# Expert weights loaded as 256 rows of 1024 columns in place of 1024 rows of 256

## Chip, core and metric

The kernel runs on one core of a Trainium2 chip. The metric is the time of one execution on the device in microseconds. The engines are PE (TensorE: matmuls, with PEld for its weight loads), DVE (VectorE), ACT (ScalarE), POOL (GpSimd) and SP (SyncE, which issues most transfers).

## The reference

One decoder layer for 1024 tokens of width 1024: a mixer (attention beside gated linear attention), and then a feed-forward part in which a router sends each token to 4 of 32 experts. The change is in the experts alone:

```python
def expert_block(args):
    xb, e = args
    u = xb @ w_mlp1[e] + b_mlp1[e]
    x_glu = jnp.minimum(u[..., ::2], SWIGLU_LIMIT)
    x_lin = jnp.clip(u[..., 1::2], -SWIGLU_LIMIT, SWIGLU_LIMIT)
    a = x_glu * jax.nn.sigmoid(SWIGLU_ALPHA * x_glu) * (x_lin + 1)
    return a @ w_mlp2[e] + b_mlp2[e]
```

`w_mlp1[e]` is 1024 x 2048 and `w_mlp2[e]` is 1024 x 1024, both float32: 8 MB and 4 MB an expert, 384 MB for all 32. The results are weighted by the gates and summed over a token's experts.

## The kernel before

All up to about 551 us is the mixer, the router and the lists of tokens. Then comes the expert stage, up to 1972 us, and a tail that finishes the rows.

An expert's tokens are gathered from memory by POOL (L1079, `xg`), turned by PE (`pxh`, L1071) and copied by ACT and DVE into `xTh` and `xTl`, the high and the low fp16 piece of the turned tokens. Each expert has a fixed number of token slots, from 368 down to 60 (`CAPS`); large and small experts take turns (`ORDER`).

The weights come in pieces of 1 MB through `piece` (L1044). It loads 1024 rows by 256 columns into a staging tile `st` of [128, 8, 256] floats, so that one partition receives eight runs of 256 floats (1 KB each). Seven staging tiles take turns. Each is split into two fp16 tiles of [128, 8, 256]: ACT writes the high piece `eh` (L168) and DVE the low piece `el`, the weight less its high piece (L169). Both work by half a tile, 128x1024 elements, so a load has two splits on each engine. Eight pairs of `eh` and `el` take turns.

```python
        return (nc.scalar.activation(dh, src, AF.Copy, scale=SW),
                nc.vector.scalar_tensor_tensor(dl, src, SW, dh, op0=OP.mult, op1=OP.subtract))
```

One pair of pieces serves 48 matmuls: 2 outputs by 8 contraction tiles by the 3 products of `mm3` (L149 to L151). In the first layer (`up`) eight pieces an expert give `pu`, from which ACT makes `gl` (L1115) and `sg` (L1117), DVE makes `lin` in three steps (L1119 to L1121), and POOL splits that into `aTh` and `aTl`. In the second layer (`down`) four pieces give `pyv`, which ACT copies to `yT` (L1146, L1148); later PE turns it, ACT scales it by the gates into `yo` (L1160), and POOL adds it to the rows of the result by an indirect transfer (L1163).

The second layer of expert i follows the first layer of expert i+1, and the turning of tokens and results goes between the pieces of the first layer. So 12 pieces with few slots (a `down` and an `up`) and 12 with many take turns.

A scheduler sets the order of each engine's instructions when the kernel is built; on the chip each engine runs in that order and waits where it must. A load is issued by SP when the staging tile that it takes has been read by both splits of its last use; a split waits for its load and for the last matmul that reads the pair of tiles it overwrites.

Of the kernel before, what the change touches and what calls it, by code (L numbers as in the profile page):

```python
# [19 lines left out]
T = 1024  # L20
D = 1024
# [5 lines left out]
SLOTS = 1152            # slot-table rows of one expert (1024 tokens at most, and one block of padding)  # L27
DUMP = 512              # rows that unused slots add zeros to, each slot of an expert's blocks to another

SW = 2048.0             # weights are split into fp16 pieces of SW * w  # L30
SX = 16.0               # activations into pieces of SX * x
SA = 256.0              # expert activations into pieces of SA * a
# [4 lines left out]
# slots per expert, by the expert's place in the order of their loads; what does not fit goes  # L37
# through the loop over overflow blocks
# [3 lines left out]
# a large and a small expert by turns, and pairs of many slots beside pairs of few; the first has two blocks  # L42
# [7 lines left out]
def layer_kernel(  # L50
# [39 lines left out]
    # ---------------------------------------------------------------- constants  # L90
# [18 lines left out]
    mt = consts.tile([128, 32], F32, name="mt")      # expert ids along the free axis  # L109
# [4 lines left out]
    cnt = consts.tile([128, NE], F32, name="cnt")    # tokens of each expert so far, on every partition  # L114
# [11 lines left out]
    pr = consts.tile([64, 2, NE], F32, name="pr")    # experts by rank, loads by rank  # L126
    Pf = consts.tile([64, NB], F32, name="Pf")       # one-hot of each block's expert
    bi = consts.tile([NB, 1], I32, name="bi")

    def rstd_from(ss, dst, width, m=128):  # L130
        """dst = (ss / width + eps) ** -0.5"""
        nc.scalar.activation(dst, ss, AF.Ln, bias=epsc[:m], scale=1.0 / width)
        nc.scalar.activation(dst, dst, AF.Exp, scale=-0.5)

    def rms(ss, rs, t2, m, after=()):
        """rs = (ss / D + eps) ** -0.5, with a step of Newton's"""
# [10 lines left out]
    def mm3(ps, sh, sl, mh, ml, first, last):  # L147
        """ps += (sh + sl)^T (mh + ml), all but the product of the two low parts"""
# [4 lines left out]
    hTh = mixer.tile([128, 8, T], F16, name="hTh")   # pieces of h, then of the heads' outputs, feature-major  # L153
# [4 lines left out]
    # pieces of q and k: those of key head g's queries on top of one another beside the key's high piece twice  # L158
# [12 lines left out]
    # ---------------------------------------------------------------- pass 1: modulation, input projection  # L171
    with tc.tile_pool(name="p1", bufs=1) as p1, tc.tile_pool(name="stage", bufs=4) as stage, \
# [4 lines left out]
        # rows -> columns: c, b_ada, g_pre_mix, g_post_mix, g_pre_ffn, g_post_ffn, g_gla_norm  # L177
# [11 lines left out]
        # silu(c)  # L189
# [9 lines left out]
        # x / rms(x), feature-major, in the places of q and of the GLA's q and k  # L199
# [23 lines left out]
        # shift1 and scale1 as columns, two at a time; s1 = (1 + scale1) g SX, sh1 = shift1 SX  # L223
# [11 lines left out]
        def ada_columns(pc):  # L235
# [8 lines left out]
            # the sums over the partitions' 8 rows: shift1's by TensorE, scale1's by VectorE  # L244
# [22 lines left out]
        def modulate(pc):  # L267
            """h = x / rms(x) * s1 + sh1 in two fp16 pieces"""
# [28 lines left out]
        def queries(p):  # L297
            # heads 2p, 2p+1 beside heads 2p+4, 2p+5: partitions 0-63 carry key head 0, 64-127 key head 1
# [22 lines left out]
        def first_queries(pc):  # L321
            """what features 256 pc to 256 pc + 255 of h add to the queries of heads 0, 1, 4 and 5"""
# [49 lines left out]
        # k, v and the low-rank gate  # L372
# [36 lines left out]
    # ---------------------------------------------------------------- pass 2: attention and GLA, by token tile  # L409
# [3 lines left out]
    # w_out: rows of attention heads i and i+4 make contraction tile i  # L413
# [622 lines left out]
    with tc.tile_pool(name="stB", bufs=7, reuse_waits="tile") as stB, tc.tile_pool(name="sp", bufs=8, reuse_waits="tile") as sp, \  # L1036
# [53 lines left out]
        def up(n, w1e, bc, xT, tag, behind=(), between=(), lead=None, wp=None):  # L1090
# [4 lines left out]
            for j in range(8):  # L1095
                with ExitStack() as es:
                    for ins in behind[:2 * j]:
                        es.enter_context(tc.issue_after(ins))
# [374 lines left out]
```

## Time and profile before

| | us |
|---|---|
| time, median of 3 runs | 2048.79 (2048.52 to 2051.15) |
| span of the profiled execution | 2046.8 |
| PE busy | 1858.8 (91%) |
| DVE busy | 1545.4 (76%) |
| ACT busy | 1307.3 (64%) |
| POOL busy | 984.7 (48%) |
| splits on DVE (L169, `el`), 768 | 936.5 |
| splits on ACT (L168, `eh`), 768 | 797.6 |
| weight loads (L1047), 384 of 1 MB | 73.7% of the DMA engines' span, with all else on their queue |

The profiled execution's own time is its span, and the table shows the median of the runs beside it. An engine's busy share is over the whole span, of which the expert stage is some two thirds; a window is a stretch of the span, with the busy time of each engine in it, the clock that TensorE was granted (1.00 is full) and the share of the DMA engines' time that packets took. That share can come out above 1.

### The profile page before, as it was taken

What the parts mean: (1) busy time and instruction counts of PE and PEld (TensorE: products, weight loads), DVE (VectorE), ACT (ScalarE), POOL (GpSimd) and SP (SyncE); (2) the same over time, 40 slices, a digit from 0 to 9 for tenths busy, and PEclk for the clock granted to TensorE, in tenths of its full rate; (3) what the DMA queues carried; (4) which work ended last, traced back from release to release, by engine and by line L of the source; (5) the groups of instructions that cost most, each with busy time, mean ns of one, the idle gap of its engine ahead of it and who ended that gap; (6) DMA issues with size and microseconds to landing.
All of it is one profiled execution on the core that took longest, in us unless ns stands there. A gap on an engine that the chain in (4) does not pass through costs nothing. (4 is left out here: it accounts for less than half of the span.)

```text
span 2046.8 us, 55660 instructions
## 1 busy us (share of the span) xinstructions
PE 1858.8 (91%) x22929; PEld 1596.1 (78%) x22929; DVE 1545.4 (76%) x2518; ACT 1307.3 (64%) x2248; POOL 984.7 (48%) x986
## 2 busy tenths in 40 slices
PE   6999999988598999989989999999999999899971
PEld 3456777655387999989989997779889999889970
DVE  6814555666679989988988996679687978969863
ACT  5524444433366868777777885678577768858760
POOL 2205765736645556545544563336344435734432
PEclk9999999999788999989999999999999999999985
DMA  8412322343399999999999999699999999999993
GB/s 287 147 45 83 94 73 83 93 151 125 135 335 320 337 330 330 339 324 337 320 312 344 337 329 331 191 316 330 312 290 308 346 298 311 327 303 313 310 278 103
DMA packets 493381, 525.94 MB, mean 257 GB/s; under 512 B 19071, under 2 KB 472969, under 8 KB 493090
## 3 DMA queue, kind: packets, MB, share of 16 engines
q1 hardware_dynamic: 474432, 476.40, 73.7%
q0 software_dynamic: 17392, 41.72, 8.7%
q8 instruction: 181, 2.97, 0.6%
q10 hardware_dynamic: 1298, 4.21, 0.5%
q14 instruction: 78, 0.64, 0.1%
HBM read 482.50 MB, written 39.76 MB: 255 GB/s over the span
## 5 line engine op out<-in xcount | busy, mean ns | idle before, releaser
L169 DVE SCALAR_TENSOR_TENSOR el<-st,eh 128x1024 f16<-128x1024 f32 x768 | 936.5, 1238 | 113.5 <-ACT eh L168 110.7
L168 ACT ACTIVATE eh<-st 128x1024 f16<-128x1024 f32 x768 | 797.6, 1054 | 284.2 <-PE pu L150 142.6
L149 PE MATMUL pu<-xTh,eh 128*128 128x232 f16 (+31 forms) x4096 | 781.8, 232 | 10.2 <-issue 4.9
L151 PE MATMUL pu<-xTh,el 128*128 128x232 f16 (+31 forms) x4096 | 781.1, 231 | 8.3 <-issue 8.2
L150 PE MATMUL pu<-xTl,eh 128*128 128x232 f16 (+31 forms) x4096 | 780.8, 231 | 4.0 <-issue 3.6
L150 PEld LDWEIGHTS <-eh 128*128 128x128 f16 x6080 | 598.8, 99 | 67.9 <-issue 46.0
L149 PEld LDWEIGHTS <-eh 128*128 128x128 f16 x6080 | 596.5, 99 | 32.5 <-issue 10.5
L151 PEld LDWEIGHTS <-el 128*128 128x128 f16 x6080 | 596.2, 99 | 29.3 <-issue 7.5
L1122 POOL CAST aTh<-lin 128x232 f16<-128x232 f32 (+31 forms) x256 | 294.0, 1148 | 538.9 <-DVE lin L1121 493.4
L149 PE MATMUL pyv<-aTh,eh 128*128 128x232 f16 (+30 forms) x1984 | 382.2, 234 | 32.6 <-ACT yT L1148 30.6
L150 PE MATMUL pyv<-aTl,eh 128*128 128x232 f16 (+30 forms) x1984 | 381.8, 233 | 2.7 <-issue 2.6
L151 PE MATMUL pyv<-aTh,el 128*128 128x232 f16 (+30 forms) x1984 | 381.7, 233 | 1.3 <-issue 1.3
L1123 POOL TENSOR_TENSOR aTl<-lin,aTh 128x232 f16<-128x232 f32 (+31 forms) x256 | 251.2, 981 | 20.7
L1119 DVE TENSOR_SCALAR lin<-pu,bt 128x232 f32<-128x232 f32 (+31 forms) x256 | 110.0, 430 | 93.5 <-PE pu L151 62.6
L1163 POOL DMA_INDIRECT yacc<-yo,tokI x52 | 94.0, 1808 | 119.1 <-ACT yo L1160 113.2
L636 POOL TENSOR_TENSOR st<-st,sil 128x512 f32<-128x512 f32 x64 | 68.3, 1068 | 150.3 <-DMA st<-in_w_ada_dram 149.7
L1115 ACT ACTIVATE gl<-pu,bt 128x232 f32<-128x232 f32 (+31 forms) x256 | 97.3, 380 | 55.4 <-PE pu L151 44.3
L1120 DVE SCALAR_TENSOR_TENSOR lin<-lin,bt,sg 128x232 f32<-128x232 f32 (+31 forms) x256 | 104.2, 407 | 14.2 <-issue 0.2
L1117 ACT ACTIVATE sg<-gl,c 128x232 f32<-128x232 f32 (+31 forms) x256 | 107.5, 420 | 1.1
L1079 POOL DMA_INDIRECT xg<-h2d,gatI x50 | 71.9, 1438 | 43.2 <-DVE gcol L1239 20.1
L1121 DVE SCALAR_TENSOR_TENSOR lin<-gl,lin 128x232 f32<-128x232 f32 (+31 forms) x256 | 84.9, 332 | 4.3
L151 PE MATMUL pb<-wvh,hTl 128*128 128x256 f16 x256 | 70.7, 276 | 0.0
(402 smaller groups left out, 2479.2 us busy)
## 6 DMA issues: line engine op xcount, KB each, us to landing
st<-in_w_mlp_dram SPq DMA_DIRECT2D x384, 1024.0 KB
st<-in_w_ada_dram SPq DMA_DIRECT2D x64, 256.0 KB
xt<-in_x_dram SPq DMA_DIRECT2D x16, 512.0 KB
st<-in_w_ada_dram SPq DMA_DIRECT2D x16, 512.0 KB
st<-in_w_in_dram SPq DMA_DIRECT2D x7, 1024.0 KB
x1d<-xt SPq DMA_DIRECT2D x8, 512.0 KB
h2d<-h2s SPq DMA_DIRECT2D x8, 512.0 KB
yacc<-yi ACTq DMA_DIRECT2D x8, 512.0 KB
```

What stands on the lines that cost most here:

```text
L149: nc.tensor.matmul(ps, sh, mh, start=first, stop=False)
L150: nc.tensor.matmul(ps, sh, ml, start=False, stop=False)
L151: return nc.tensor.matmul(ps, sl, mh, start=False, stop=last)
L168: return (nc.scalar.activation(dh, src, AF.Copy, scale=SW), nc.vector.scalar_tensor_tensor(dl, src, SW, dh, op0=OP.mult, op1=OP.subtract))
L169: nc.vector.scalar_tensor_tensor(dl, src, SW, dh, op0=OP.mult, op1=OP.subtract))
L1115: nc.scalar.activation(gl, pu[0], AF.Relu, scale=-SG, bias=bc(0, j))
L1117: sgs.append(nc.scalar.activation(sg, gl, AF.Sigmoid, scale=-1.702 * INV / SG, bias=c7))
L1119: nc.vector.tensor_scalar(lin, pu[1], bc(1, j), bc(2, j), op0=OP.max, op1=OP.min)
L1120: nc.vector.scalar_tensor_tensor(lin, lin, bc(3, j), sg, op0=OP.add, op1=OP.mult)
L1122: nc.gpsimd.tensor_copy(aTh[:, j, :], lin)
L1123: lows.append(nc.gpsimd.tensor_tensor(aTl[:, j, :], lin, aTh[:, j, :], op=OP.subtract))
L1163: end["dma"] = nc.gpsimd.indirect_dma_start(out=yacc, out_offset=bass.IndirectOffsetOnAxis(ap=si(b)[:m, :], axis=0), in_=yo[:m, :], in_off ...
```

## The change

`piece` becomes `pieces`, which loads a group of four pairs at once. Each of its four loads fetches 256 rows by 1024 columns into a staging tile of [128, 2, 1024] floats: two runs of 1024 floats (4 KB each) for a partition. Each load holds a quarter of the rows for all four pairs, so it is split into four parts, 128x512 elements each, one for each pair. A group has the same 4 MB and the same four loads, with 16 splits on each engine in place of 8, and a pair is complete when all four loads are in. The numbers of staging tiles (7) and of pairs (8) stay.

`up` calls `pieces` for its pieces 0 to 3 and again for 4 to 7, `down` once. The pieces taken ahead of the first tokens are a whole group where they were one piece. The staging tile is also borrowed for the first-layer biases (`b1f`) and for rows of the tail (`xys`), in its new shape. The matmuls are the same, in number and in shape.

```diff
-        def piece(src):
-            st = stB.tile([128, 8, 256], F32, name="st")
-            loads.append(nc.sync.dma_start(st, src.rearrange("o (k p) f -> p (o k) f", p=128)))
-            wh = sp.tile([128, 8, 256], F16, name="eh")
-            wl = sp.tile([128, 8, 256], F16, name="el")
-            for hh in range(2):
-                ks = slice(hh * 4, hh * 4 + 4)
-                splits.append(split(wh[:, ks, :], wl[:, ks, :], st[:, ks, :]))
-            return wh, wl
+        def pieces(src, j):
+
+            ws = [(sp.tile([128, 8, 256], F16, name="eh"), sp.tile([128, 8, 256], F16, name="el")) for _ in range(4)]
+            for kq in range(4):
+                st = stB.tile([128, 2, 1024], F32, name="st")
+                rows = src[:, kq * 256:(kq + 1) * 256, j * 1024:(j + 1) * 1024]
+                loads.append(nc.sync.dma_start(st, rows.rearrange("o (k p) f -> p (o k) f", p=128)))
+                ks = slice(kq * 2, kq * 2 + 2)
+                for c, (wh, wl) in enumerate(ws):
+                    splits.append(split(wh[:, ks, :], wl[:, ks, :], st[:, :, c * 256:(c + 1) * 256]))
+            return ws
...
-                    wh, wl = wp if wp and j == 0 else piece(w1e(j))
+                if j % 4 == 0:
+                    with ExitStack() as es:
+                        for ins in behind[:2 * j]:
+                            es.enter_context(tc.issue_after(ins))
+                        ws = wp if wp and j == 0 else pieces(w1e(j), j // 4)
+                wh, wl = ws[j % 4]
...
+                if half == 0:
+                    ws = pieces(w2e, 0)
                 for q in range(2):
-                    wh, wl = piece(w2e(half * 2 + q))
+                    wh, wl = ws[half * 2 + q]
...
-        wp = piece(w1[ds(e[0], 1), :, 0:256])
+        wp = pieces(w1[ds(e[0], 1)], 0)
...
-            b1f = stB.tile([128, 8, 256], F32, name="st")[0:NE].rearrange("p a n -> p (a n)")
+            b1f = stB.tile([128, 2, 1024], F32, name="st")[0:NE].rearrange("p a n -> p (a n)")
```

The order moves in three places that matter below. The names in brackets are the queues and engines that a row waits for. First, ACT at the start of the expert stage, where the first expert's first pieces stand beside its tokens, before:

```order
L168 ACTIVATE eh<-st 128x1024 [waits DMAHW2_49,DVE_49]
L168 ACTIVATE eh<-st 128x1024
L1075 ACTIVATE xTh<-pxh 128x8x128 [waits PE_49]
L1075 ACTIVATE xTh<-pxh 128x8x104 [waits PE_49]
L168 ACTIVATE eh<-st 128x1024 [waits DMAHW5_49,Pool_49]
L168 ACTIVATE eh<-st 128x1024
```

and after:

```order
L168 ACTIVATE eh<-st 128x512 [waits DMAHW2_49,DVE_49]
L168 ACTIVATE eh<-st 128x512 [waits DMAHW5_49,Pool_49]
L168 ACTIVATE eh<-st 128x512
L168 ACTIVATE eh<-st 128x512 [waits DMAHW7_49]
L168 ACTIVATE eh<-st 128x512 [waits DMAHW4_49]
L168 ACTIVATE eh<-st 128x512 x3
L168 ACTIVATE eh<-st 128x512 [waits DMAHW5_49]
L168 ACTIVATE eh<-st 128x512 x3
L168 ACTIVATE eh<-st 128x512 [waits DMAHW6_49]
L168 ACTIVATE eh<-st 128x512 x3
L1076 ACTIVATE xTh<-pxh 128x8x128 [waits PE_49]
L1076 ACTIVATE xTh<-pxh 128x8x104 [waits PE_49]
```

Two splits stood ahead of the two copies of the tokens (`xTh`), and now 16 stand there, four for each of four loads, load by load (the waits for DMAHW2, 4, 5 and 6 at the head of each four).

Second, ACT in the first layer of the expert with 112 slots, at its first three pieces, before:

```order
L168 ACTIVATE eh<-st 128x1024 [waits DMAHW5_49,PE_49]
L1115 ACTIVATE gl<-pu,bt 128x112 [waits DVE_49,PE_49]
L1160 ACTIVATE yo<-pxy,gcol 92x512 [waits DMASW6_49,PE_49]
L1117 ACTIVATE sg<-gl,c_78 128x112 [waits Activation_49]
L168 ACTIVATE eh<-st 128x1024
L168 ACTIVATE eh<-st 128x1024 [waits DMAHW6_49,PE_49]
L1115 ACTIVATE gl<-pu,bt 128x112 [waits DVE_49,PE_49]
L1160 ACTIVATE yo<-pxy,gcol 92x512 [waits PE_49]
L1117 ACTIVATE sg<-gl,c_78 128x112 [waits Activation_49]
L168 ACTIVATE eh<-st 128x1024
L168 ACTIVATE eh<-st 128x1024 [waits DMAHW7_49,PE_49]
L1115 ACTIVATE gl<-pu,bt 128x112 [waits DVE_49,PE_49]
```

and after:

```order
L168 ACTIVATE eh<-st 128x512 [waits DMAHW5_49,PE_49]
L1118 ACTIVATE gl<-pu,bt 128x112 [waits DVE_49,PE_49]
L1165 ACTIVATE yo<-pxy,gcol 92x512 [waits DMASW6_49,PE_49]
L1120 ACTIVATE sg<-gl,c_78 128x112 [waits Activation_49]
L168 ACTIVATE eh<-st 128x512 [waits DMAHW6_49]
L168 ACTIVATE eh<-st 128x512 [waits DMAHW7_49]
L1118 ACTIVATE gl<-pu,bt 128x112 [waits DVE_49,PE_49]
L1165 ACTIVATE yo<-pxy,gcol 92x512 [waits PE_49]
L1120 ACTIVATE sg<-gl,c_78 128x112 [waits Activation_49]
L168 ACTIVATE eh<-st 128x512 x3
L168 ACTIVATE eh<-st 128x512 [waits DMAHW0_49]
L1118 ACTIVATE gl<-pu,bt 128x112 [waits DVE_49,PE_49]
```

Where each piece had one load to wait for, the first loads of the group come at once, the second pair's splits of them next, and the split that waits for the fourth load (DMAHW0) follows only after these, with two rounds of `gl` and `sg` in between.

Third, ACT in the first layer of the expert with 216 slots, at the same place, before:

```order
L168 ACTIVATE eh<-st 128x1024 [waits DMAHW1_49,PE_49]
L1115 ACTIVATE gl<-pu,bt 128x216 [waits DVE_49,PE_49]
L1160 ACTIVATE yo<-pxy,gcol 128x512 [waits DMASW3_49,PE_49]
L1117 ACTIVATE sg<-gl,c_78 128x216 [waits Activation_49]
L168 ACTIVATE eh<-st 128x1024
L168 ACTIVATE eh<-st 128x1024 [waits DMAHW2_49,PE_49]
```

and after:

```order
L168 ACTIVATE eh<-st 128x512 [waits DMAHW1_49,DVE_49,PE_49]
L1118 ACTIVATE gl<-pu,bt 128x216 [waits PE_49]
L1165 ACTIVATE yo<-pxy,gcol 128x512 [waits DMASW3_49,PE_49]
L1120 ACTIVATE sg<-gl,c_78 128x216 [waits Activation_49]
L168 ACTIVATE eh<-st 128x512 [waits DMAHW2_49]
L168 ACTIVATE eh<-st 128x512 [waits DMAHW3_49]
L168 ACTIVATE eh<-st 128x512 [waits DMAHW4_49]
L168 ACTIVATE eh<-st 128x512 [waits DVE_49,PE_49]
L1118 ACTIVATE gl<-pu,bt 128x216 [waits PE_49]
```

Here the first pair's four splits, of all four loads (DMAHW1 to 4), follow one another, with no other split between.

## Rows read from the trace of the kernel before

**Rows 1.** The page: the span and the queue of all weight loads.

```profile
span 2046.8 us, 55660 instructions
...
q1 hardware_dynamic: 474432, 476.40, 73.7%
```

**Rows 2.** Windows by pair of experts: start and end, length, busy us (instructions) per engine, clock, share.

```profile
core 0: us, PE busy (x) PEld busy (x) DVE busy (x) ACT busy (x) POOL busy (x), PEclk, DMA share, GB/s
568.80:666.90 98.10, 87.94 (x1045) 83.44 (x1045) 84.09 (x145) 65.92 (x91) 48.03 (x39) 0.89 1.09 328
666.90:745.80 78.90, 74.50 (x1227) 73.98 (x1225) 73.43 (x99) 64.46 (x97) 45.31 (x38) 0.98 1.09 332
745.80:831.60 85.80, 84.58 (x1228) 84.01 (x1226) 74.30 (x100) 64.49 (x97) 44.77 (x38) 1.00 1.08 332
831.60:916.00 84.40, 76.60 (x1227) 76.04 (x1225) 74.17 (x99) 64.52 (x97) 43.51 (x38) 0.94 1.07 330
...
998.20:1084.50 86.30, 77.36 (x1227) 76.81 (x1225) 74.86 (x101) 64.62 (x97) 40.95 (x38) 0.96 1.07 322
...
1166.40:1248.00 81.60, 78.68 (x1243) 77.88 (x1241) 74.28 (x100) 65.42 (x98) 48.33 (x39) 1.00 1.09 338
1248.00:1366.70 118.70, 116.43 (x1228) 82.08 (x1226) 77.64 (x101) 69.36 (x103) 38.32 (x38) 0.99 0.86 271
1366.70:1442.40 75.70, 73.08 (x1265) 72.15 (x1264) 72.27 (x100) 66.12 (x101) 48.45 (x41) 0.98 1.05 315
...
1548.80:1623.90 75.10, 72.05 (x1267) 71.03 (x1266) 71.46 (x99) 65.89 (x101) 47.11 (x41) 1.00 1.05 320
...
1719.30:1804.10 84.80, 75.38 (x1234) 74.67 (x1233) 73.06 (x99) 65.59 (x99) 49.33 (x39) 0.94 1.05 317
...
sum 1403.70, PE 1336.62 PEld 1259.77 DVE 1186.13 ACT 1045.65 POOL 692.11; mean PE 83.54 PEld 78.74 DVE 74.13 ACT 65.35 POOL 43.26
```

**Rows 3.** Windows: loads of x in rows of 4 KB, then of weights in rows of 1 KB.

```profile
10.00:14.00 4.00, 3.50 (x16) 2.59 (x14) 2.45 (x7) 3.74 (x10) 0.00 (x0) 1.00 0.99 393
...
826.00:844.00 18.00, 18.00 (x229) 17.97 (x227) 14.48 (x17) 12.20 (x18) 4.36 (x4) 1.00 1.10 348
```

**Rows 4.** Timeline of ACT, 896 to 912: start, duration, instruction, idle before it.

```profile
897.16 1.06 ACT L168 ACTIVATE eh<-st 128x1024 f16<-128x1024 f32 x1 [5.46 <-DMA st<-in_w_mlp_dram]
...
902.21 1.06 ACT L168 ACTIVATE eh<-st 128x1024 f16<-128x1024 f32 x1 [2.53 <-DMA st<-in_w_mlp_dram]
```

**Rows 5.** Timeline of PE, 905 to 907.

```profile
906.57 0.30 PE L149 MATMUL pyv<-aTh,eh 128*128 128x168 f16 x1 [7.37 <-ACT yT L1148]
```

**Rows 6.** Waits of the DMA queue of SP: who for whom, us, times, longest.

```profile
SPq L1047 <- DVE el L169: 588.9, 217, 8.5
```

**Rows 7.** Instructions of line 169 (DVE), duration ns least, median, most.

```profile
L169 DVE SCALAR_TENSOR_TENSOR el<-st,eh x768: 1190/1218/1902, 559.3 to 1968.4; 128x1024 f16<-128x1024 f32 x192
...
L169 DVE SCALAR_TENSOR_TENSOR wol<-wo,woh x16: 639/844/1527, 186.2 to 404.1; 128x512 f16<-128x512 f32 x16
```

**Rows 8.** Instructions of line 168 (ACT), likewise.

```profile
L168 ACT ACTIVATE eh<-st x768: 1039/1054/1109, 558.2 to 1965.2; 128x1024 f16<-128x1024 f32 x192
...
L168 ACT ACTIVATE woh<-wo x16: 629/630/632, 167.6 to 379.4; 128x512 f16<-128x512 f32 x16
```

**Rows 9.** Timeline of ACT at the start of the expert stage.

```profile
563.49 1.02 ACT L1075 ACTIVATE xTh<-pxh 128x1024 f16<-128x1024 f16 x1 [3.32 <-PE pxh L1071]
567.89 0.86 ACT L1075 ACTIVATE xTh<-pxh 128x832 f16<-128x832 f16 x1 [3.38 <-PE pxh L1071]
...
571.79 2.00 ACT L168 ACTIVATE eh<-st 128x1024 f16<-128x1024 f32 x2 [1.15 <-DMA st<-in_w_mlp_dram]
```

**Rows 10.** Timeline of PE, 558 to 568.8.

```profile
566.98 1.57 PE L1071 MATMUL pxh<-identh,xg 104*128 104x104 f16 x16 [2.68 <-DMA xg<-h2d,gat]
```

**Rows 11.** Timeline of SP at the start of the program.

```profile
1.58 6.29 SPq L316 DMA_DIRECT2D xt<-in_x_dram  x8
```

**Rows 12.** Timeline of ACT at the start of the program.

```profile
5.28 1.06 ACT L209 ACTIVATE junk<-xt 128x1024 f16<-128x1024 f32 x1 [3.26 <-DMA xt<-in_x_dram]
```

More of the change, by code (lines that the diff above doesn't have):

```diff
@@ L1095, in up @@
             for j in range(8):
-                with ExitStack() as es:
-                    for ins in behind[:2 * j]:
-                        es.enter_context(tc.issue_after(ins))
-                    wh, wl = wp if wp and j == 0 else piece(w1e(j))
+                if j % 4 == 0:
[4 more added lines that the diff above has]
+                wh, wl = ws[j % 4]
                 if n <= 256:
@@ L1196, in piece_of @@
                         e[1] = expert(i, perm1)
-                return w1[ds(e[min(j, 1)], 1), :, j * 256:(j + 1) * 256]
+                return w1[ds(e[min(j, 1)], 1)]
             return up(CAPS[r], piece_of,
@@ L1304, in layer_kernel @@
             _, si, gc = args(ORDER[i])
-            yTs = down(n, lambda q: w2[ds(e[1], 1), :, q * 256:(q + 1) * 256], aT)
+            yTs = down(n, w2[ds(e[1], 1)], aT)
             left = combine(n, yTs, si, gc)
@@ L1315, in layer_kernel @@
         aTh, aTl = up_of(i, e, xT[i][0])
-        wps = [piece(w2[ds(e[1], 1), :, q * 256:(q + 1) * 256]) for q in range(4)]
+        wps = pieces(w2[ds(e[1], 1)], 0)
         with tc.issue_after(sgs[-1].ins):
@@ L1333, in layer_kernel @@
             if t < NT - 2:
-                st = stB.tile([128, 8, 256], F32, name="st").rearrange("p a n -> p (a n)")
+                st = stB.tile([128, 2, 1024], F32, name="st").rearrange("p a n -> p (a n)")
                 xys.append((st[:, 0:D], st[:, D:2 * D]))
@@ L1426, in layer_kernel @@
             run(steps)
-            aTo = up(128, lambda j: w1[ds(e, 1), :, j * 256:(j + 1) * 256],
+            aTo = up(128, lambda j: w1[ds(e, 1)],
                      lambda q, j: bto[:, q, j, :], xTo, "B")
-            yTo = down(128, lambda q: w2[ds(e, 1), :, q * 256:(q + 1) * 256], aTo)
+            yTo = down(128, w2[ds(e, 1)], aTo)
             run(combine(128, yTo, lambda b: ti[:, 0:1], lambda b: gx))
```

## The prediction

> **What bounds the kernel now.** I read the page's busy shares, then the windows of the expert stage pair by pair, then the waits, and at last single instructions. The span is 2046.8 us [rows 1]; the median of the runs is 2048.8, so 2.0 us lie around the span. The change touches only the expert weights, so 0 to 551 us (the mixer) and the tail after 1972 us stay as they are.
>
> The expert stage alternates an expert of many slots with one of few, and it repeats every two experts, so a window holds one such pair: 24 loads of 1 MB, 48 splits on ACT and 48 on DVE, and 24 pairs of pieces for PE. The 16 windows make 1403.7 us, of which PE is busy 1336.6 [rows 2]: PE idles 67 us, and where it has idled its clock falls, which the granted clock shows (0.89, 0.94, 0.96). The loss by the clock is (1 − clock) × length. Four windows are **starved** (78.9, 84.4, 86.3 and 84.8 us, 334.4 together): PE idles 4.4, 7.8, 8.9 and 9.4 us = 30.6 in them and loses 1.6 + 5.1 + 3.5 + 5.1 = 15.3 by the clock. Four **middle** ones (82 to 86 us, the first and the last are shown) idle 0.7 to 2.9, 7.6 in all. The others are heavy (PE is the bound), follow a heavy one, or are the first and the last.
>
> What starves PE is the weight DMA. Its share stands at 1.05 to 1.09 in the starved windows [rows 2], and at 348 GB/s with 1.10 in a stretch without a pause [rows 3]: 316 GB/s for each unit of share. The page gives the same: 476.40 MB in 73.7% of 2046.8 us is 316 GB/s, or 3.32 us of all engines for one 1 MB load [rows 1]. 24 × 3.32 = 79.7 us is about the length of the starved windows. Just ahead of such a stop, ACT waits 5.46 and 2.53 us for `st` before a split [rows 4], and PE then stands 7.37 us [rows 5]; the profile names `yT`, but ACT was done with splits just before, and the weights are the late party. DVE is busy 73.1 to 74.9 us of the same windows [rows 2]: it is the next bound, close behind.
>
> **The change, part by part.**
>
> *Transfer.* Rows of 1 KB become rows of 4 KB. The trace has those: x is loaded in rows of 4 KB, at 393 GB/s with a share of 0.99 [rows 3], 397 GB/s, 2.64 us for 1 MB. I take 2.64 (3.32 is the other end, if the pitch between the rows should cost what their length saves). A window then needs 24 × 2.64 = 63.4 us for weights in place of 79.7, and its share falls to about 0.86. The DMA is no longer the bound.
>
> [...]
>
> *Splits.* A group of four pairs took 8 splits of 128x1024 on each of DVE and ACT and takes 16 of 128x512. On DVE 128x1024 takes 1190 ns at least (median 1218), and 128x512, in the mixer, 639 at least (median 844) [rows 7]. Two small for one large cost 2 × 639 − 1190 = 88 ns more, 48 times in a window: **+4.2 us**. With the 28 ns that the median of the large one stands over its minimum on each instruction, 116 ns: +5.6. With the median of the small ones, 2 × 844 − 1218 = 470 ns: +22.6; that is an upper bound, since those 16 ran beside other work of the mixer, and I take the lower. DVE in a starved window goes from 73.9 (mean of the four) to 78.1 to 79.5. On ACT: 2 × 629 − 1054 = 204 ns [rows 8] × 48 = +9.8 at most, 65 → 75, which lies under DVE's.
>
> [...]
>
> *So DVE takes the DMA's place.* DVE also idles a little: in the windows that follow a heavy one, 75.7 and 75.1, it idles 3.4 and 3.6 [rows 2]. Between 78.1 + 0 and 79.5 + 3.5 I take 81 us for each starved window.
>
> *Order.* A pair of pieces now needs all four loads of its group. The loads of a group are let go together: with 7 staging buffers the fourth load of the next group goes into the buffer of this group's first, which is free only when the last pair's split of it is done. SP waits 588.9 us for `el` already, without harm where loads are queued ahead [rows 6]. I cost this at 0, since while the load is away DVE has the last pair's other splits and the next group's first ones to do; the price without that cover is rival C.
>
> *Start.* In the first group the order stands load by load, and all 16 splits stand ahead of both copies of the first tokens. Now the copies end at 568.75 and the first product follows at 568.8. The third load's split started at 571.79 [rows 9], with 3.25 MB landed (the biases too). The fourth: 571.79 + 0.75 × 2.64 − 2 × (3.32 − 2.64) = 572.4. Then four splits of ACT (2.5), a copy (1.02), the transposes of the second block (half of 1.57 [rows 10], whose 16 operations are eight for each piece), its copy (0.86): first product about 577.5, **8.7 us later**. The first window idles 10.2 us and loses 10.8 by the clock; with a whole group ready that should shrink by about as much. DVE allows an earlier end: its 84.09 us of the window, 2.4 for the two splits that now run before it and 5 for the price above, less the 16 × 0.64 = 10.2 us of splits that are done by 574.9, leave 81.3, and 3 idle make 659 against 666.9. So the term lies between −8 and +8.7; I take 0.
>
> *Sum.* Starved: 4 × 81 = 324 against 334.4: −10.4. Middle: half of their 7.6: −4. Heavy, after heavy, last: 0, since PE bounds them or eight pairs stand ready. First: 0. Span 2046.8 − 14 = 2032, plus 2.0 around it makes 2034, rounded up to **2035 us**.
>
> **The rivals.**
>
> *B, full relief.* DVE's idle vanishes, since splits run ahead in heavy windows, and PE bounds all. The four give back 30.6 + 15.3, the middle 7.6 and the first 6: 59.5, so **1989**. For it: eight pairs of pieces can be ready ahead, and DVE could work for the next window while PE is the bound in a heavy one. Against: eight are a third of a window's 24, and in the four PE alone would need 70 to 74 us (its busy time less the loss by the clock), less than DVE's 78.
>
> *C, slower: the fourth load's round trip.* Load to load: x's first 512 KB was issued at 1.58 and used at 5.28, 3.7 us [rows 11, 12], of which 1.3 is the transfer at 2.64 a MB; so 2.4 + 2.64 = 5.0 for a whole load, plus 0.6 for ACT's split: 5.6. DVE's cover, where its order goes straight on (the 216 slots in the order shown), is three splits of the old group and three of the new: 6 × 0.64 = 3.8. It then stops 1.8 us a group, six groups a window: 79 + 10.8 = 90. Eight windows (the starved and the middle, 666 us) become 718: +52, **2101**; where it stops in half of the groups, 8 × 84.4 = 675: +9, 2058. It decides from 0.7 us a group, where 79 + 6 × 0.7 reaches their mean of 83.2. Against: in the expert of 112 slots the second pair's three splits stand ahead of the fourth load's, 9 × 0.64 = 5.8, which covers it. For: only one spare load of room, and ACT's and PE's part in the chain is not counted.
>
> *D, no change.* The price is 136 ns a pair of splits, not 88: 73.9 + 6.5 + 3.5 = 84, 4 × 84 = 336 against 334: **2049**.
>
> *E, it doesn't load faster.* The rows of one load are 8 KB apart in memory for the first layer. Then 24 × 3.32 stays, with DVE at 79 beside it: between D and C; its chance is in theirs.
>
> **How the numbers follow.** A measurement of this kernel tells 0.2%, 4 us, from no change. Forecast (DVE the bound, 5 to 35 us gained): 0.44. B: 0.16. C, whole or half: 0.28. D: 0.12. Faster: the forecast less 0.04 that falls under 4 us or turns out a loss, plus B: 0.56. Same: D and half of that 0.04: 0.14. Slower: C and the other half: 0.30. The range reaches from B's value, 1988, to 2078, between C's half and its whole; some 0.1 is left out on either side.
>
> **What would show it.** Right: share of DMA under 0.95 in the starved windows, weights at 380 GB/s or more for each unit of share; DVE busy 78 to 80 us in them with 128x512 at 640 to 670 ns; PE idle less than now, clock at 0.97 or more. C: splits on ACT waiting for `st` once a group, on the fourth load, and SP waiting for `el` right before it. Start: first product near 577. Wrong altogether: DVE's 128x512 at over 700 ns, or the load still at 3.3 us.

## The result, and the profile after

The changed kernel takes **2146.1 us** (median of 4 runs, 2134.4 to 2148.1) against 2048.7 us before: a ratio of 1.046, 95% interval 1.043 to 1.049. The forecast was 2035 us with a range up to 2078. It is slower, and by more than the rival that ended on this side.

The page of the changed kernel, lines that answer to [rows 1] and to the busy times in the table ahead (the groups of instructions: busy time, mean ns | idle time before them and what ended most of it):

```profile
span 2145.8 us, 57143 instructions
...
PE 1884.6 (88%) x22929; PEld 1612.4 (75%) x22929; DVE 1616.1 (75%) x3286; ACT 1373.8 (64%) x3016; POOL 917.7 (43%) x986
...
q1 hardware_dynamic: 179520, 476.40, 63.5%
...
L169 DVE SCALAR_TENSOR_TENSOR el<-st,eh 128x512 f16<-128x512 f32 x1536 | 1026.8, 711 | 132.3 <-ACT eh L168 129.4
L168 ACT ACTIVATE eh<-st 128x512 f16<-128x512 f32 x1536 | 875.4, 622 | 330.5 <-DMA st<-in_w_mlp_dram 209.9
```

The transfers did get shorter: 63.5% of 2145.8 us for the same 476.40 MB is 350 GB/s for each unit of share (316 before), 3.00 us for a 1 MB load in place of 3.32. The splits cost about what was reckoned: DVE 1026.8 us in place of 936.5, ACT 875.4 in place of 797.6. What is new stands behind the bar of the last line: ACT now idles before its splits mostly for the weight loads.

The same pairs of experts as in [rows 2], seven of the 16 lines, and the sum:

```profile
593.80:686.80 93.00, 85.67 (x1044) 81.78 (x1044) 80.84 (x184) 63.45 (x131) 42.76 (x39) 0.91 0.88 304
686.80:771.20 84.40, 74.24 (x1227) 73.69 (x1225) 75.52 (x144) 66.04 (x141) 38.71 (x38) 0.98 0.95 319
771.20:865.70 94.50, 86.66 (x1227) 85.22 (x1225) 82.54 (x153) 71.40 (x150) 33.81 (x38) 0.96 0.90 305
865.70:955.60 89.90, 76.22 (x1228) 75.79 (x1226) 78.06 (x147) 69.02 (x145) 44.23 (x37) 0.94 0.90 302
...
1046.00:1130.50 84.50, 79.01 (x1226) 78.28 (x1224) 77.11 (x146) 68.06 (x144) 34.86 (x38) 0.96 0.94 317
...
1428.90:1512.10 83.20, 74.06 (x1266) 72.37 (x1264) 74.79 (x143) 67.20 (x143) 50.36 (x40) 0.98 0.92 306
...
1810.20:1897.60 87.40, 76.94 (x1235) 76.22 (x1233) 74.84 (x141) 65.89 (x140) 44.13 (x39) 0.92 0.90 296
...
sum 1482.20, PE 1352.26 PEld 1270.85 DVE 1249.72 ACT 1109.11 POOL 627.68; mean PE 84.52 PEld 79.43 DVE 78.11 ACT 69.32 POOL 39.23
```

The share of DMA has fallen below 0.96 in all of them, to 0.90 to 0.95 in the starved ones, where the forecast had about 0.86, and yet all of the 16 but the first and the one from 1046.0 are longer. By the groups of the prediction: starved 334.4 → 346.2 (+11.8), middle 331.5 → 361.7 (+30.2), first 98.1 → 93.0 (−5.1), and the seven that it costed at nothing (heavy, after heavy, last) 639.7 → 681.3 (+41.6); together +78.5. The first product starts at 593.8 in place of 568.8, of which 13.1 us lie after the first slots' numbers are known (28.6 us from there, 15.5 before). The other 11.9 lie in the mixer, whose instructions are the same, in the same order; in the profiles of this study it ends anywhere between 546 and 565 us, for kernels that share it. The tail gave back 4.5. 78.5 + 13.1 + 11.9 − 4.5 is the 99.0 between the spans. From the first slots' numbers to the end, which leaves the mixer out, the profile takes 1580.6 us in place of 1493.5.

The waits of 600 us to the end (who <- for whom: us, times, longest), before and then after:

```profile
ACT eh L168 <- DMA st<-in_w_mlp_dram: 65.3, 47, 6.8
...
PE pyv L149 <- ACT yT L1148: 30.6, 9, 7.4
```

```profile
ACT eh L168 <- DMA st<-in_w_mlp_dram: 196.6, 119, 7.8
...
PE pyv L149 <- ACT yT L1153: 77.9, 26, 10.9
```

ACT waits three times as long for loads. PE's idle time in the 16 windows has grown from 67.1 to 129.9 us, and 47 of these 63 us are its waits for `yT` at `pyv`. How the one leads to the other is seen at the longest stop. ACT, 926 to 946 us, in the window of the experts with 168 and 112 slots (start, duration, instruction, idle before it and what ended it):

```profile
926.35 1.24 ACT L168 ACTIVATE eh<-st 128x512 f16<-128x512 f32 x2
935.38 0.63 ACT L168 ACTIVATE eh<-st 128x512 f16<-128x512 f32 x1 [7.78 <-DMA st<-in_w_mlp_dram]
935.91 0.34 ACT L1118 ACTIVATE gl<-pu,bt 128x112 f32<-128x112 f32 x1
...
943.81 2.18 ACT L168 ACTIVATE eh<-st 128x512 f16<-128x512 f32 x4
945.89 0.43 ACT L1153 ACTIVATE yT<-pyv 128x336 f32<-128x336 f32 x1
```

And PE there, and then DVE:

```profile
935.27 0.24 PE L151 MATMUL pyv<-aTh,el 128*128 128x168 f16 x1
946.37 0.30 PE L149 MATMUL pyv<-aTh,eh 128*128 128x168 f16 x1 [10.86 <-ACT yT L1153]
```

```profile
936.36 0.39 DVE L1122 TENSOR_SCALAR lin<-pu,bt 128x112 f32<-128x112 f32 x1 [6.79 <-ACT gl L1118]
```

From 926.35 ACT makes the first two of a pair's four splits, and then waits 7.78 us for the load of the third. In its order behind that split stand the activation `gl` (935.91) and then, behind more splits, the copy `yT` (945.89). PE has two PSUM tiles for `pyv`; both are full at 935.5, and it goes on at 946.37, 0.48 us after `yT` has begun to free one. The pieces for that product, counted off in the timelines of ACT and DVE from the start of the stage, had been split by 929 us. So PE stands still not for its weights but for a copy that waits its turn behind a split whose load is late. DVE stands 6.79 us too, for the `gl` behind the same split.

Loads are held back by the way staging tiles come free. SP's issues from 900 to 923 us, and then from 920 to 943:

```profile
899.69 15.20 SPq L1050 DMA_DIRECT2D st<-in_w_mlp_dram  x8
```

```profile
924.20 4.78 SPq L1050 DMA_DIRECT2D st<-in_w_mlp_dram  x4
```

Four loads go out within 4.78 us, and no other in these 23 us. In the scheduler's order a group's splits go pair by pair, so that the four tiles of a group are read to the end only with its last pair; four loads are then issued at once, and the next must wait for the next group's last pair. Here the four landed one after another, with the last updates of their semaphores at 939.1, 941.6, 944.1 and 946.6, and the next load went out at 944.58.

This burst is not what made the 7.78 us, though. The load waited for there, the third of its group, is the last of the eight that SP had issued by 914.9; of the 16 updates of its semaphore, 12 had come by 927.5 and the last only at 935.4. From 920 to 938 the queue of POOL's indirect transfers took 23% of the engines' time; whether they held up the last four parts was not tested. The fourth load of the group, one of the four issued from 924.20, kept ACT another 1.04 us at 939.1.

That groups matter is seen in the sum. Sorted by the load whose semaphore the split waits for, ACT's 196.6 us fall on the first to the fourth load of a group as 6, 37, 72 and 78 us (4 are not sorted); in the kernel before, the 65.3 us fall on its loads, taken by fours, as 14, 21, 15 and 15.

### The profile page after: what moved, and what is told of

Same layout as the page of the kernel before. It is cut to its first block, busy times and chain, and to the rows that moved or that the text cites. A ratio compares the mean times of both kernels' runs of the same rounds, so it can differ in the third digit from the quotient of the medians.

```text
span 2145.8 us, 57143 instructions
## 1 busy us (share of the span) xinstructions
PE 1884.6 (88%) x22929; PEld 1612.4 (75%) x22929; DVE 1616.1 (75%) x3286; ACT 1373.8 (64%) x3016; POOL 917.7 (43%) x986
## 3 DMA queue, kind: packets, MB, share of 16 engines
q1 hardware_dynamic: 179520, 476.40, 63.5%
## 5 line engine op out<-in xcount | busy, mean ns | idle before, releaser
L169 DVE SCALAR_TENSOR_TENSOR el<-st,eh 128x512 f16<-128x512 f32 x1536 | 1026.8, 711 | 132.3 <-ACT eh L168 129.4
L168 ACT ACTIVATE eh<-st 128x512 f16<-128x512 f32 x1536 | 875.4, 622 | 330.5 <-DMA st<-in_w_mlp_dram 209.9
L149 PE MATMUL pyv<-aTh,eh 128*128 128x232 f16 (+30 forms) x1984 | 391.4, 238 | 88.3 <-ACT yT L1153 77.9
L150 PE MATMUL pyv<-aTl,eh 128*128 128x232 f16 (+30 forms) x1984 | 391.0, 237 | 0.0
L151 PE MATMUL pyv<-aTh,el 128*128 128x232 f16 (+30 forms) x1984 | 390.8, 237 | 0.0
L1126 POOL TENSOR_TENSOR aTl<-lin,aTh 128x232 f16<-128x232 f32 (+31 forms) x256 | 198.1, 774 | 20.8
L1168 POOL DMA_INDIRECT yacc<-yo,tokI x52 | 87.4, 1680 | 154.4 <-ACT yo L1165 78.6
L636 POOL TENSOR_TENSOR st<-st,sil 128x512 f32<-128x512 f32 x64 | 68.4, 1069 | 156.5 <-DVE e L559 96.8
L1072 PE MATMUL pxh<-identh,xg 128*128 128x128 f16 (+27 forms) x848 | 55.2, 206 | 45.5 <-ACT xTh L1076 17.4
L1080 POOL DMA_INDIRECT xg<-h2d,gatI x50 | 66.4, 1329 | 50.2 <-DVE gcol L1244 32.0
```

The lines of the kernel that those rows point to most:

```text
L149: nc.tensor.matmul(ps, sh, mh, start=first, stop=False)
L150: nc.tensor.matmul(ps, sh, ml, start=False, stop=False)
L151: return nc.tensor.matmul(ps, sl, mh, start=False, stop=last)
L168: return (nc.scalar.activation(dh, src, AF.Copy, scale=SW), nc.vector.scalar_tensor_tensor(dl, src, SW, dh, op0=OP.mult, op1=OP.subtract))
L1126: lows.append(nc.gpsimd.tensor_tensor(aTl[:, j, :], lin, aTh[:, j, :], op=OP.subtract))
L1168: end["dma"] = nc.gpsimd.indirect_dma_start(out=yacc, out_offset=bass.IndirectOffsetOnAxis(ap=si(b)[:m, :], axis=0), in_=yo[:m, :], in_off ...
```

## The experiments

All but the first and the last change the kernel after; ratios are to the kernel before, with their 95% intervals. Theory H is that the held staging tiles are the cause, theory S that the doubled splits are.

### The doubled splits alone

The kernel before, with

```diff
-            for hh in range(2):
-                ks = slice(hh * 4, hh * 4 + 4)
+            for hh in range(4):
+                ks = slice(hh * 2, hh * 2 + 2)
```

> The kernel before with each 1 MB load (1024 rows by 256 columns, as before) split into four parts of 128x512 on ACT and DVE in place of two of 128x1024. It takes the doubled splits alone, without the group of four. Theory H (hold): what costs time in the changed kernel is that the four staging tiles of a group are let go together, so that loads go out in bursts and the last lands late; then this kernel, where each tile is let go by itself, is within 1% of the kernel before, 2045 to 2068 us. Theory S (split price): the 71 us of DVE and 66 us of ACT that the halved splits added are what the changed kernel lost; then this one is at 2110 to 2150 us.

2053.5 us, 1.0025 (1.0005 to 1.0044), as H expected. Its page:

```profile
span 2051.2 us, 57123 instructions
...
q1 hardware_dynamic: 474432, 476.40, 73.7%
...
L169 DVE SCALAR_TENSOR_TENSOR el<-st,eh 128x512 f16<-128x512 f32 x1536 | 1024.2, 711 | 75.0 <-ACT eh L168 72.5
```

It has the DVE work of the changed kernel (1024.2 us) with the DMA work of the kernel before, and pays 5 us, where loads are the bound. With the next but one, which has the same splits beside the long runs, S falls.

### Groups of two

A load fetches 512 rows by 512 columns:

```diff
-            for kq in range(4):
-                st = stB.tile([128, 2, 1024], F32, name="st")
-                rows = src[:, kq * 256:(kq + 1) * 256, j * 1024:(j + 1) * 1024]
+            for kq in range(2):
+                st = stB.tile([128, 4, 512], F32, name="st")
+                rows = src[:, kq * 512:(kq + 1) * 512, j * 512:(j + 1) * 512]
...
-                ks = slice(kq * 2, kq * 2 + 2)
+                ks = slice(kq * 4, kq * 4 + 4)
...
```

> The changed kernel with groups of two: a load fetches 512 rows by 512 columns (runs of 2 KB), two loads feed two pairs, with splits of 128x1024, as many as in the kernel before. Theory H: bursts of two in place of four leave at most a third of the loss, 2030 to 2080 us. Theory S: no price at all, 2030 to 2049 us. If neither hold nor splits were the cause but the long runs themselves, it would lie halfway, near 2095 us.

**2011.3 us, 0.982 (0.979 to 0.984)**: faster than both kernels, and below what either theory expected (2030 us and more). Its page and its wait for loads:

```profile
span 2008.8 us, 55645 instructions
...
PE 1842.7 (92%) x22929; PEld 1585.2 (79%) x22929; DVE 1541.2 (77%) x2518; ACT 1302.8 (65%) x2248; POOL 991.0 (49%) x986
...
q1 hardware_dynamic: 277824, 476.40, 68.4%
```

```profile
ACT eh L168 <- DMA st<-in_w_mlp_dram: 41.2, 23, 7.4
```

68.4% of 2008.8 us is 347 GB/s, 3.02 us a load: runs of 2 KB bring nearly all that runs of 4 KB bring (3.00), with no more splits than before, and ACT waits less for loads than in the kernel before. By itself it doesn't part H from S, since it takes both away.

### The splits in the order of the loads

The changed kernel, each split scheduled after the one before it in the order of the code, so that the four splits of a load follow one another:

```diff
+                    with ExitStack() as es:
+                        for ins in splits[-1:]:
+                            es.enter_context(tc.issue_after(ins[0].ins))
+                            es.enter_context(tc.issue_after(ins[1].ins))
-                    splits.append(split(wh[:, ks, :], wl[:, ks, :], st[:, :, c * 256:(c + 1) * 256]))
+                        splits.append(split(wh[:, ks, :], wl[:, ks, :], st[:, :, c * 256:(c + 1) * 256]))
...
```

> The changed kernel with its splits kept in the order of the loads on ACT and DVE: the four splits of a load follow one another, so that its staging tile is free as soon as they are done, not with the last pair of the group. The splits are as many and as small as in the changed kernel. Theory H: most of the 78 us lost in the windows of the expert stage comes back, 2070 to 2105 us (the later start of the stage, 13 us, stays), and ACT's wait for the weight loads falls from 197 us to under 100. Theory S: no gain, 2135 to 2150 us. Against H: a load's splits now need the tiles of all four pairs of two groups ago, so PE's lead falls from eight pairs towards four, which may give up to half of it back.

2046.0 us, 0.9985 (0.9966 to 1.0004): 100 us less than the changed kernel, with the same loads and the same splits, and better than the 2070 to 2105 us that H expected. It is not told apart from the kernel before. Its waits, and the windows of two starved pairs, of a middle one between them, and the sum; the profiled execution (2037.7 us) is the fastest of ten:

```profile
PE pyv L151 <- DVE el L169: 20.0, 14, 2.8
...
ACT eh L168 <- DMA st<-in_w_mlp_dram: 13.6, 14, 2.5
...
PE pyv L149 <- ACT yT L1157: 1.3, 3, 0.6
```

```profile
670.40:746.80 76.40, 73.12 (x1227) 72.33 (x1225) 73.89 (x143) 68.01 (x145) 41.67 (x37) 1.00 1.00 336
746.80:834.80 88.00, 84.58 (x1226) 83.87 (x1224) 80.30 (x152) 68.57 (x145) 49.75 (x40) 1.00 0.97 330
834.80:912.80 78.00, 74.05 (x1226) 73.36 (x1225) 74.60 (x145) 67.93 (x145) 43.42 (x37) 1.00 1.00 346
...
sum 1384.50, PE 1326.24 PEld 1246.48 DVE 1223.90 ACT 1095.86 POOL 743.66; mean PE 82.89 PEld 77.91 DVE 76.49 ACT 68.49 POOL 46.48
```

The wait for loads has fallen from 196.6 us to 13.6, below what H asked for, and PE's for `yT` from 77.9 to 1.3. What PE waits for most at `pyv` are now DVE's low pieces (20.0 us). The starved windows are at 76.4 and 78.0 us, shorter than the forecast's 81. DVE makes 143 and 145 instructions in them, 44 and 46 more than before [rows 2], and 52 more in the middle window, where the doubled splits alone are 48: some of its work is done a window early. The sum, 1384.5, is 19 below the 1403.7 of [rows 2], in a run 8 us faster than the median. The first product still comes 28.9 us after the first slots' numbers, as late as in the changed kernel.

### One staging tile more, and one fewer

Eight staging tiles beside seven pairs of pieces (the same memory), and six beside eight:

```diff
-    with tc.tile_pool(name="stB", bufs=7, reuse_waits="tile") as stB, tc.tile_pool(name="sp", bufs=8, reuse_waits="tile") as sp, \
+    with tc.tile_pool(name="stB", bufs=8, reuse_waits="tile") as stB, tc.tile_pool(name="sp", bufs=7, reuse_waits="tile") as sp, \
...
-    with tc.tile_pool(name="stB", bufs=7, reuse_waits="tile") as stB, tc.tile_pool(name="sp", bufs=8, reuse_waits="tile") as sp, \
+    with tc.tile_pool(name="stB", bufs=6, reuse_waits="tile") as stB, tc.tile_pool(name="sp", bufs=8, reuse_waits="tile") as sp, \
```

> The changed kernel with eight staging tiles in place of seven, and seven pairs of pieces in place of eight (the same memory). With eight, the fourth load of a group takes the tile that its own like of two groups ago gave back, and is no longer bound to the first split of the last pair of the group just ahead of it. Theory H (hold): the fourth load comes in time, 2050 to 2100 us, and ACT's wait for the weight loads falls under 120 us. Rival L (lead): what the changed kernel lacks are pairs ready ahead of PE, and then one pair fewer makes it slower, 2150 us or more.

> The changed kernel with six staging tiles in place of seven, all else the same. Theory H: two loads of each group instead of one wait for the last pair of the group ahead, so the loss grows, 2180 to 2260 us, and ACT's wait for the loads with it, to 260 us or more. Rival L: the pairs ready ahead are the same eight, 2140 to 2160 us.

Eight: 2087.8 us, 1.019 (1.014 to 1.024). Six: 2188.7 us, 1.068 (1.062 to 1.074); two runs each. The waits with eight tiles, and then with six:

```profile
ACT eh L168 <- DMA st<-in_w_mlp_dram: 136.4, 74, 6.9
...
PE pyv L149 <- ACT yT L1153: 37.3, 19, 8.2
```

```profile
ACT eh L168 <- DMA st<-in_w_mlp_dram: 318.6, 148, 6.6
...
PE pyv L149 <- ACT yT L1153: 105.6, 26, 9.7
```

With 6, 7 and 8 tiles ACT waits 318.6, 196.6 and 136.4 us for loads, and the time follows (2189, 2146, 2088), though with eight there is a pair fewer ready ahead. Both times lie where H had them and outside L's ranges, so in this kernel it is not a lack of ready pairs. H's wait for six (260 us or more) was met, that for eight (under 120) was not. Sorted as above, the third and the fourth load of a group take 178 and 97 us with six tiles, 72 and 78 with seven, 42 and 84 with eight: the third's part follows the tiles, but the eighth tile did not bring the fourth load in time. Whether a tile more helps the kernel before as well was not run.

### A third PSUM tile for the second layer

```diff
-            tc.tile_pool(name="psU", bufs=4, space=PSUM, reuse_waits="tile") as psU, \
-            tc.tile_pool(name="psV", bufs=2, space=PSUM, reuse_waits="tile") as psV, \
+            tc.tile_pool(name="psU", bufs=3, space=PSUM, reuse_waits="tile") as psU, \
+            tc.tile_pool(name="psV", bufs=3, space=PSUM, reuse_waits="tile") as psV, \
```

> The changed kernel with three PSUM tiles for the second layer's sums (pyv) in place of two, and three for the first layer's (pu) in place of four. Theory B (blocked copies): PE stops in the second layer not for weights but because ACT's copy yT, which frees a PSUM tile, stands in ACT's order behind splits that wait for late loads; a third tile lets PE run on, so PE's wait for yT (88 us) falls under 50 and the time to 2100 to 2135 us. Rival W: the weights themselves are missing there, and the profile's naming of yT is only the last of several waits: 2140 to 2160 us, the idle time staying under another name.

2109.3 us, 1.030 (1.028 to 1.032; two runs), 37 us less, with the loads as late as they were; 11 of the 36 us between the two profiles lie in the mixer:

```profile
ACT eh L168 <- DMA st<-in_w_mlp_dram: 236.5, 126, 6.9
...
PE pxy L1164 <- ACT yT L1153: 25.8, 14, 5.5
PE pyv L149 <- ACT yT L1153: 24.6, 12, 6.9
```

ACT waits even longer for its loads (236.5 us), but PE's wait for `yT` at `pyv` is 24.6 us in place of 77.9, as theory B expected. Part of it has moved to the turning of the results (`pxy`), which needs the same late copy: 25.8 us, where it was 1.7. So the last link at `pyv` is a full PSUM tile and not missing weights, and the copy is late as before.

### Whole groups in one tile

The pieces of a group in one tile of 1024 columns each for `eh` and `el`, two such tiles in turn, and two splits of 128x1024 a load:

```diff
...
-            ws = [(sp.tile([128, 8, 256], F16, name="eh"), sp.tile([128, 8, 256], F16, name="el")) for _ in range(4)]
+            wh, wl = sp.tile([128, 8, 1024], F16, name="eh"), sp.tile([128, 8, 1024], F16, name="el")
+            ws = [(wh[:, :, c * 256:(c + 1) * 256], wl[:, :, c * 256:(c + 1) * 256]) for c in range(4)]
...
-                for c, (wh, wl) in enumerate(ws):
-                    splits.append(split(wh[:, ks, :], wl[:, ks, :], st[:, :, c * 256:(c + 1) * 256]))
+                for k in range(2):
+                    splits.append(split(wh[:, kq * 2 + k, :], wl[:, kq * 2 + k, :], st[:, k, :]))
...
```

> The changed kernel's loads (256 rows by 1024 columns), but the pieces of a group stand in one tile of 1024 columns for each of eh and el, two such tiles taking turns, and a load is split in two parts of 128x1024 (one row of each run) in place of four of 128x512. It has the long runs and the group of four, no doubled splits, and each staging tile is let go by itself; PE's lead now moves by whole groups. Theory H with the price of the splits on top: that price is 4 us a window for DVE, so it lies at or below the kernel with the splits in the order of the loads, 2010 to 2046 us. Rival L: whole groups must be done before their tile comes free, 2060 us or more.

2103.2 us, 1.026 (1.022 to 1.031), outside what H expected and where rival L had it. The waits:

```profile
PEld L151 <- DVE el L169: 84.9, 97, 3.6
...
ACT eh L168 <- DMA st<-in_w_mlp_dram: 9.9, 6, 2.5
```

The loads come in time (9.9 us), but now PE does wait for the low pieces, since a tile comes free only when PE is done with a whole group. Freed staging tiles are not enough; the pairs ahead matter too, once they move by fours. In the changed kernel they still move one by one.

### The start

The first expert's tokens turned after the first load's splits:

```diff
-        with tc.issue_after(splits[-1][0].ins), tc.issue_after(splits[-1][1].ins):
+        with tc.issue_after(splits[3][0].ins), tc.issue_after(splits[3][1].ins):
```

> The changed kernel with the first expert's tokens turned after the first load's splits in place of after the whole first group. The first product, at 593.8 us (568.8 before), should come about 12 us earlier. Both theories: 2132 to 2137 us if the gain stays to the end; 2146 if the stage is bound by something that starts no earlier, the loads and splits.

2129.4 us, 1.039 (1.036 to 1.042), 17 us less by the medians, more than expected. Its first product:

```profile
576.90 0.93 PE L149 MATMUL pu<-xTh,eh 128*128 128x232 f16 x4 [0.29 <-ACT xTh L1076]
```

That is 20.1 us after the first slots' numbers, 8.5 less than in the changed kernel; the rest of the 17 us lies in the mixer, which ended 8.4 us earlier in this profile and is not touched.

### Two mends together, and others

The splits in the order of the loads, as above, and with that

```diff
-        with tc.issue_after(splits[-1][0].ins), tc.issue_after(splits[-1][1].ins):
+        with tc.issue_after(splits[3][0].ins), tc.issue_after(splits[3][1].ins):
```

> Both mends of the changed kernel at once: its splits in the order of the loads, and the first tokens turned after the first load's splits. The second alone gave 17 us and the first 100; if they add up, 2029 to 2037 us, and so about 0.7% faster than the kernel before, as the prediction had it. If the earlier start is given back, since the stage here is bound by loads and splits, 2040 to 2046.

2042.2 us, 0.996 (0.994 to 0.999): faster than the kernel before, by 0.4%, but only 4 us better than the order of the loads alone, which five and ten runs, spread over 13 and 18 us, don't tell apart. It lies where the expectation had it if the earlier start is given back. The first product comes 20.1 us after the first slots' numbers in place of 28.9, and from these numbers to the end the two profiles take 1486.3 and 1484.3 us: the earlier start brought nothing here.

Groups of two, as above, and with that

```diff
+                    with ExitStack() as es:
+                        for ins in splits[-1:]:
+                            es.enter_context(tc.issue_after(ins[0].ins))
+                            es.enter_context(tc.issue_after(ins[1].ins))
```

> Groups of two (512 rows by 512 columns, splits of 128x1024) with the splits kept in the order of the loads. Theory H: a hold of two costs something too, so it gains on the kernel with groups of two in the scheduler's order, 1995 to 2008 us. If a hold of two is covered, it stays at 2011 within 5 us.

2011.1 us, 0.982 (0.978 to 0.987), no different from groups of two in the scheduler's order. A hold of two tiles out of seven is covered.

Groups of two with

```diff
-        with tc.issue_after(splits[-1][0].ins), tc.issue_after(splits[-1][1].ins):
+        with tc.issue_after(splits[1][0].ins), tc.issue_after(splits[1][1].ins):
```

> Groups of two, with the first tokens turned after the first load's splits. First product 17.3 us after the first slots' numbers (15.5 in the kernel before), so 2 to 3 us are to be had: 2006 to 2011 us.

2014.1 us, 0.983 (0.980 to 0.986), above what was expected: nothing gained either.

### The third PSUM tile in the kernel before

The same edit of `psU` and `psV`, made in the kernel before:

```diff
-            tc.tile_pool(name="psU", bufs=4, space=PSUM, reuse_waits="tile") as psU, \
-            tc.tile_pool(name="psV", bufs=2, space=PSUM, reuse_waits="tile") as psV, \
+            tc.tile_pool(name="psU", bufs=3, space=PSUM, reuse_waits="tile") as psU, \
+            tc.tile_pool(name="psV", bufs=3, space=PSUM, reuse_waits="tile") as psV, \
```

> The kernel before with three PSUM tiles for pyv and three for pu. The prediction read PE's stop of 7.37 us in the starved windows of this kernel as a lack of weights, against the profile, which names ACT's copy yT. Theory B: the profile was right, and the copy stood behind splits that waited for loads; then PE's wait for yT (30.6 us) falls under 15, and the time to 2020 to 2042 us. Rival W (the prediction's reading): the loads alone are the bound, the time stays at 2043 to 2055 us whatever PE's waits are called.

2040.8 us, 0.9974 (0.9953 to 0.9994), at the edge of what theory B expected:

```profile
ACT eh L168 <- DMA st<-in_w_mlp_dram: 121.6, 97, 7.7
...
PE pxy L1159 <- ACT yT L1148: 12.8, 7, 3.5
PE pyv L149 <- ACT yT L1148: 10.4, 5, 4.2
```

PE's wait for `yT` at `pyv` fell from 30.6 us to 10.4, while that at `pxy` rose from 3.1 to 12.8. The profile had named the right cause in [rows 5]: counted off in the trace of the kernel before, the pair for that product had been split by 886.4 us, 20 us ahead of it. But the time fell by only 5 to 8 us: ACT waits 121.6 us for loads where it waited 65.3, and PE waits 17.8 us for `lin` before a `pu` where it waited 4.9, with a `pu` tile fewer. That fits the loads as the bound there, with the blocked copy as the way by which they reached PE; the run doesn't price the blocked copy alone.

## Why the prediction was wrong

**The step that failed** is the one on the order: "I cost this at 0, since while the load is away DVE has the last pair's other splits and the next group's first ones to do". This priced the held tiles at nothing, and asked the wrong engine. On ACT the activations and copies that PE and its PSUM tiles wait for stand in the same order as the splits, and a split that waits for its load stops them all; at the stop shown DVE did not run on either, but stood 6.79 us for ACT's `gl`. In place of 0 the 16 windows lost 78.5 us, with ACT's wait for loads up from 65.3 to 196.6 us and PE's for `yT` from 30.6 to 77.9. With the splits in the order of the loads the windows came to 97.7 us less, and both waits to 13.6 and 1.3. The runs with 6, 7 and 8 tiles and with a third PSUM tile show the links: held tiles, late loads, blocked copies, a PE that stands.

**What bounds the kernel now.** Right that the loads did [rows 3], and half wrong on how they stopped PE: the text overruled the profile's `yT` in [rows 5] by the argument that ACT was done with splits just before and the weights were the late party. Splits that wait in front of a copy were the very mechanism; read as the profile had it, it could have led to the price of a late load on ACT.

**Transfer.** 2.64 us a load was right for an undisturbed stretch of the changed kernel, 410 GB/s at a share of 1.03:

```profile
672.00:680.00 8.00, 6.94 (x71) 6.69 (x70) 7.72 (x13) 3.90 (x7) 1.07 (x2) 1.00 1.03 410
```

That is 398 GB/s, 2.63 us. Over the whole run the queue made it 3.00, so the term was 0.36 us too good, 9 us a window, and the 350 GB/s missed the 380 that the forecast gave as a sign. The share of DMA stood below 0.96, so the transfers did not fill a window; what a shorter load would have saved of ACT's waits was not tested.

**Splits.** Well sized. DVE's price is 90.3 us of busy time over 768, 118 ns (forecast 88 to 116), ACT's 77.8 us, 101 ns (at most 204 forecast). One split takes DVE 711 ns on average, over the 700 that the forecast called a sign of being wrong altogether; splits that follow one another overlap (17 take 10.3 us on DVE from 945.4, 606 ns each), so that the price in busy time stayed at 118 ns all the same. Rival D's 136 ns for a pair of small splits is shown by no run; the changed kernel gave 118. With the splits in the order of the loads the starved windows are at 74 to 79 us with DVE busy 73 to 75, less than the forecast's 78 to 79.5, since part of its work is done in other windows, as rival B had it. PE's longest wait at `pyv` there is for DVE's low pieces (20.0 us): the forecast's next bound does appear once the loads come in time.

**Start.** 13.1 us in place of 8.7: the fourth load's splits came later than reckoned, 18.3 us after the first load's:

```profile
570.50 2.19 ACT L168 ACTIVATE eh<-st 128x512 f16<-128x512 f32 x4 [1.58 <-DMA st<-in_w_mlp_dram]
...
588.81 2.19 ACT L168 ACTIVATE eh<-st 128x512 f16<-128x512 f32 x4 [3.37 <-DMA st<-in_w_mlp_dram]
590.90 1.00 ACT L1076 ACTIVATE xTh<-pxh 128x1024 f16<-128x1024 f16 x1
592.85 0.86 ACT L1076 ACTIVATE xTh<-pxh 128x832 f16<-128x832 f16 x1 [0.94 <-PE pxh L1072]
```

The first window gave 5.1 back, so the term is +8, at the end of its bounds, where 0 was taken.

**Heavy windows at 0.** Wrong: +41.6 us over seven windows, of which the four heavy ones took 18.6, the two after a heavy one 16.3 and the last 6.7. "PE bounds them" holds only as long as nothing else stops PE: in the heavy window that lost most (11.2 us) PE stood 8.0 us at once for `yT`. What the other three lost isn't traced.

**The rivals.** C had the cause, the seven tiles, and nearly the place: the third load made ACT wait nearly as long as the fourth (72 and 78 us). For its eight windows it had nearly the price, +52 reckoned and +42 measured, partly by luck, since it counted DVE's stops and not ACT's. It left out the seven others and the start, and so ended at 2101. Its chance of 0.28 had been held down by an argument that counted splits on DVE alone, and the range stopped short of C's own value. B's and the forecast's mechanism showed only where the hold was taken away.

**Open.** How much of the 100 us that the order of the loads brought comes from earlier loads and how much from copies that no longer stand behind waiting splits was not separated: the new order changes both. Nor is it shown why the last parts of the load in the stop above landed 8 us after the others, or why the eighth tile left the wait for the fourth load as it was; and the 12 us in the mixer of the changed kernel's profile have no cause shown here.

## What to carry to other kernels

When a change makes several loads feed several consumers, ask when each staging tile is read for the last time in the order that the scheduler makes, and price a late load on every engine that has a consumer of it in its order, with all that stands behind it there. Half the change may have all its gain: groups of two took the long runs without doubled splits and with a hold that seven tiles cover. And where the profile names a releaser, test the name before overruling it.

## What the runs showed of the hardware

The queue of the weight loads moved 347 GB/s for each unit of share over the whole run with rows of 2 KB and 350 with rows of 4 KB, nearly the same, against 316 with 1 KB; 403 of its 476 MB are expert weights. Half-size splits cost little: 118 ns of busy time for two small ones over one large on DVE (1026.8 us in all against 936.5), 101 on ACT (875.4 against 797.6).
